# Hybrid encoder layer on one core: a new list of stage priorities for the list scheduler

## The chip, the core and the metric

The kernel runs on one core of a Trainium2 chip. A core has five engines that run their own instruction streams and meet at semaphores: PE (TensorE, matrix products; PEld are its weight loads), DVE (VectorE), ACT (ScalarE), POOL (GpSimd) and SP (SyncE, which here only issues transfers). Transfers between HBM and on-chip memory run on 16 DMA engines. The metric is the device time of one execution in microseconds (us), as a median over runs. The profile is one execution, recorded on the chip.

## What is computed

One encoder layer for 512 tokens of width 1024, everything in float32, cut to what matters:

```python
h = rmsnorm(x, mix_norm)
p = h @ w_in                                   # 1024 x 9248
rx, ry, qkv, z, ba, gates = split(p)
y_rnn = rglru_branch(rx, ry, ...) @ w_rnn_proj # gated linear recurrence, forward and backward, 1536 channels
y_dn  = deltanet_branch(qkv, z, ba, ...) @ w_dn_proj   # 8 heads, chunks of 64 tokens, both directions
g_rnn, g_dn = split(sigmoid(gates))
x = x + (g_rnn * y_rnn + g_dn * y_dn) @ w_out
h = rmsnorm(x, ffn_norm)
gt, up = split(h @ w_gate_up)                  # 1024 x 5632
x = x + (silu(gt) * up) @ w_down               # 2816 x 1024
return rmsnorm(x, final_norm)

# inside deltanet_branch, per head and chunk:
A   = strict_lower((k * beta) @ k.T * decay)
u   = solve(A + I, v * beta);  w = solve(A + I, kb * exp(gc))
# then a scan over the chunks with a 128 x 128 state
```

## The kernel before, in words

**Products.** Every large float32 product is made of three products of a reduced type (fp32r): each operand is split into a high part, cast by ACT (`whi`, `hh`), and a low part, the rest, subtracted by DVE (`wlo`, `hl`). PE then does high by high, high by low and low by high into one PSUM tile (`mm`, `st` or `ax`). So each block of 1024 x 128 weights costs one transfer into `wraw`, one ACT cast, one DVE subtraction and a few dozen matmuls, most of 512 columns. The feed-forward part (`gate_up`, L1350) works by a Strassen scheme in 20 units of 84 matmuls of 256 columns: it adds and subtracts weight blocks on DVE to save products on PE.

**The delta net** goes through four groups `g` of two heads. `dn_mats(g)` (L861) computes K by K products on PE (into an `ax` tile), and DVE writes the scaled triangular matrix into `na`. `dn_inverse(g)` (L901) inverts it: 69 DVE instructions that depend on one another (an elimination of 30 steps on 32 x 32 blocks), then on PE a dense batch of 32 x 32 matmuls (`pr`, `px`, `pz`) and of 64 x 64 ones, with ACT copies between. `dn_state(g)` (L985) goes over the chunks.

**Down projection ahead.** Ten of the Strassen units, and the plain unit before them, carry a `down_sums` (L1162): two transfers of `w_down` blocks, two DVE additions into `bg`, and one transfer of the sums back to HBM.

**What sets the order.** Nothing is issued while the Python runs. A `Plan` object (L52) records every instruction as an operation, with its engine, its estimated cost and its dependencies (`Plan.add`, L118). Calls of `spend(us)` (L439) open a new *stage*; there are 229, numbered from 0. Within a stage an operation has an offset of its own: for instance, a weight transfer is put 40 us ahead of the product that uses it. At the end `Plan.order()` (L145) makes one list of all operations by list scheduling: it steps through an estimated time, and each engine that is free takes the ready operation with the smallest key. The key is

```python
for (s, d), b in zip(self.where, self.bases):
    if s < len(TIMES):
        b, b0 = TIMES[s] * 100, b
    elif TIMES:
        b += max(TIMES) * 100 - b0
    when.append(b + d)
```

that is, `TIMES[stage] * 100` plus the offset, in ns. Stages past the end of the list keep their planned distances, behind the largest entry. On ACT a change of the function table adds `SWITCH` to the key. A key is only a rank among ready operations, not a time at which anything is meant to run. The keys also decide which tile gets a buffer first (`slots`, L187): the pools have 3 `wraw`, 2 `whi`, 2 `wlo`, 14 and 22 scratch tiles, 2 `bg` and 8 PSUM tiles.

The resulting list is emitted instruction by instruction, so that each engine's stream is fixed in that order; an engine waits where the next operand is not there. The emission has one line, so nearly every instruction of the profile carries L379, and the profile is read by tile names.

**Stages by number:** 0 to 2 norm and constants; 3 the beta and gate columns; 4 to 51 input projections, the recurrence and the first delta group's inputs, mixed; 60, 76, 92 and 110 `dn_mats` of groups 0 to 3, followed in 61, 77, 93 and 111 by `dn_inverse` and in 62, 78, 94 and 112 by `dn_state`; 125 to 141 the branch projections; 143 to 174 the output projection; 175 to 178 two plain feed-forward units; 179 to 198 the 20 Strassen units; 199 to 221 the down projection; 222 to 228 the last products, the final norm and the writes.

Of the kernel before, what the change touches and what calls it, by code (L numbers as in the profile page):

```python
# [32 lines left out]
RELEASE = 200  # L33
LOOK = 40
TIMES = [
# [10 lines left out]
]  # L46
ENGINES = ("PE", "DVE", "ACT", "POOL", "SP")
N2, N4, NW = 14, 22, 3
# [1575 lines left out]
```

## Time and profile before

| what | before |
|---|---|
| median of 3 runs | 1064.7 us (1064.27 to 1064.9) |
| the profiled execution: first to last instruction | 1066.3 us |
| granted TensorE clock, mean | 0.996 |
| PE busy | 1045.2 us (98%), 6731 matmul records |
| DVE busy | 867.6 us (81%), 1606 instructions |
| ACT busy | 675.7 us (63%), 1244 instructions |
| POOL busy | 53.0 us (5%) |
| HBM read and written | 113.78 MB and 7.90 MB |

The profiled execution's own time is its span: 1066.3 us, counted from the first to the last instruction, which stands 1.6 us above the median of the runs. In the views, a row of the timeline gives the start, the duration, the engine and the tiles (output<-inputs), with the idle time before it in brackets and what ended it. A row of the waits gives the waiting engine and tile, what was waited for, the sum in us, how often, and the longest. A row of the windows gives the stretch, its length, the busy time of each engine with the number of instructions, the granted clock of PE, the busy share of the DMA engines and the GB/s.

### The profile page before, as it was taken

To read this page: it belongs to the slowest core of one execution; us is meant where nothing else is said; L and a number is where in the kernel's file an instruction comes from. 1 tells how busy PE (TensorE), PEld (TensorE's weight loads), DVE (VectorE), ACT (ScalarE), POOL (GpSimd) and SP (SyncE) were. 2 spreads that over 40 slices of the span, in tenths; PEclk is the share of its full clock that TensorE was granted. 3 is DMA by queue.
4 is the path that set the end of the run, shared out by engine and by line. 5 is a ranking of instruction groups with operands and counts; after the bars stand their busy time and mean duration, and the time that the engine had idled before them with its cause. 6 is when DMAs were issued, how large, how long until landed. Compare 5 with 4: busy or idle time off the path is not lost.

```text
span 1066.3 us, 17661 instructions
## 1 busy us (share of the span) xinstructions
PE 1045.2 (98%) x6731; PEld 908.7 (85%) x6731; DVE 867.6 (81%) x1606; ACT 675.7 (63%) x1244; POOL 53.0 (5%) x109
## 2 busy tenths in 40 slices
PE   8999999999999999999999999999999999999997
PEld 7888888887879887988788898889999999998876
DVE  7679899669966696599379567669989989889998
ACT  7997997878464856783874534447444544546664
POOL 2000000202000211110020000000000000000000
PEclk9999999999999999999999999999999999999999
DMA  8142333224331243223203222554577433325643
GB/s 254 45 119 79 102 85 91 68 86 124 104 109 33 83 125 91 58 73 99 71 15 96 79 103 80 183 168 149 178 229 246 129 102 104 113 93 197 193 137 113
DMA packets 174390, 122.83 MB, mean 115 GB/s; under 512 B 5953, under 2 KB 160721, under 8 KB 174305
## 3 DMA queue, kind: packets, MB, share of 16 engines
q1 hardware_dynamic: 172832, 118.41, 37.1%
q10 hardware_dynamic: 1184, 3.15, 0.8%
q8 instruction: 53, 0.87, 0.3%
q0 software_dynamic: 288, 0.13, 0.1%
q14 instruction: 33, 0.26, 0.1%
HBM read 113.78 MB, written 7.90 MB: 114 GB/s over the span
## 4 chain that ended last, share of the span: by engine, by line
PE 71%; DVE 14%; ACT 8%; issue 4%; DMA 3%; POOL 0%; SPq 0%; DVEq 0%; ACTq 0%; POOLq 0%
PE mm L379 43%; PE ax L379 18%; PE st L379 10%; DVE t L379 9%; ACT t L379 5%; DVE wlo L379 3%; ACT L379 1%; DVE na L379 1%; ACT whi L379 1%; ACT ax L379 1%; DMA wraw<-sums 1%; DMA wraw<-in_w_in_dram 1%; DMA wraw<-in_w_gate_up_dram 1%; DMA bg<-in_w_down_dram 1%; DVE hl L379 0%
## 5 line engine op out<-in xcount | busy, mean ns | idle before, releaser
L379 DVE TENSOR_TENSOR t<-t,t 128x512 fp32r<-128x512 f32 (+23 forms) x466 | 226.7, 501 | 14.8 <-ACT t L379 6.3
L379 PE MATMUL mm<-hh,whi 128*128 128x512 f32 (+2 forms) x648 | 229.4, 363 | 0.4 <-ACT hh L379 0.4
L379 PE MATMUL mm<-hl,whi 128*128 128x512 f32 (+2 forms) x648 | 228.9, 362 | 0.8 <-DVE hl L379 0.8
L379 ACT CAST whi<-wraw 128x1024 fp32r<-128x1024 f32 (+3 forms) x139 | 130.1, 937 | 155.2 <-PE mm L379 87.8
L379 DVE TENSOR_TENSOR wlo<-wraw,whi 128x1024 fp32r<-128x1024 f32 (+3 forms) x138 | 150.4, 1092 | 75.1 <-PE mm L379 27.4
L379 PE MATMUL mm<-hh,wlo 128*128 128x512 f32 (+1 forms) x632 | 146.8, 364 | 0.0
L379 PE MATMUL ax<-t,t 32*32 32x32 f32 (+3 forms) x1062 | 141.7, 288 | 2.9 <-issue 1.8
L379 PEld LDWEIGHTS mm<-hl,whi 128*128 128x128 f32 (+1 forms) x648 | 121.8, 188 | 18.5 <-DVE hl L379 1.2
L379 PEld LDWEIGHTS mm<-hh,whi 128*128 128x128 f32 (+1 forms) x648 | 121.7, 188 | 17.8 <-ACT hh L379 0.7
L379 PEld LDWEIGHTS ax<-t,t 128*128 128x128 f32 (+1 forms) x1062 | 109.5, 162 | 20.9 <-issue 4.6
L379 PEld LDWEIGHTS mm<-hh,wlo 128*128 128x128 f32 x632 | 109.1, 190 | 17.4
L379 ACT CAST t<-t 128x512 fp32r<-128x512 f32 (+2 forms) x128 | 80.9, 650 | 48.2 <-DVE t L379 42.9
L379 DVE SCALAR_TENSOR_TENSOR t<-mm,par,t 128x511 f32<-128x511 f32 (+1 forms) x108 | 80.3, 745 | 20.3 <-ACT t L379 19.0
L379 PE MATMUL mm<-t,t 128*128 128x256 f32 (+1 forms) x468 | 91.6, 337 | 0.8 <-DVE t L379 0.7
L379 ACT ACT_TABLE_LOAD x69 | 88.5, 1283 | 5.2 <-PEq L1610 1.7
L379 PE MATMUL mm<-t,whi 128*128 128x512 f32 x320 | 82.1, 395 | 0.5 <-ACT whi L379 0.5
L379 PEld LDWEIGHTS mm<-t,t 128*128 128x128 f32 x468 | 72.4, 190 | 11.1 <-DVE t L379 2.5
L379 PEld LDWEIGHTS mm<-t,whi 128*128 128x128 f32 x320 | 59.3, 188 | 12.7 <-ACT whi L379 0.7
L379 ACT CAST t<-wraw 128x1024 fp32r<-128x1024 f32 (+1 forms) x51 | 44.9, 881 | 29.0 <-DMA wraw<-in_w_gate_up_dram 11.2
L379 ACT ACTIVATE t<-t 128x128 f32<-128x128 f32 (+4 forms) x86 | 47.1, 559 | 24.9 <-DVE t L379 23.6
L379 DVE TENSOR_TENSOR t<-wraw,t 128x1024 fp32r<-128x1024 f32 (+1 forms) x51 | 51.7, 1016 | 6.1 <-ACT t L379 5.9
L379 PE MATMUL mm<-t,wlo 128*128 128x512 f32 x160 | 43.3, 394 | 0.0
(210 smaller groups left out, 1702.9 us busy)
## 6 DMA issues: line engine op xcount, KB each, us to landing
wraw<-in_w_in_dram SPq DMA_DIRECT2D x72, 512.0 KB, 3.8
wraw<-in_w_gate_up_dram SPq DMA_DIRECT2D x44, 512.0 KB, 4.2
wraw<-in_w_rnn_proj_dram SPq DMA_DIRECT2D x16, 384.0 KB, 3.6
bg<-in_w_down_dram SPq DMA_DIRECT2D x11, 512.0 KB, 4.1
sums<-bg SPq DMA_DIRECT2D x11, 512.0 KB, 4.7
wraw<-sums SPq DMA_DIRECT2D x11, 512.0 KB, 4.6
wraw<-in_w_down_dram SPq DMA_DIRECT2D x22, 256.0 KB, 3.0
wraw<-in_w_down_dram SPq DMA_DIRECT2D x11, 512.0 KB, 3.7
```

Of the source, the lines that this page charges most:

```text
L379: self.plan.add(e, lambda: real(*a, **kw), outs, ins, cost, tail, table)
```

## The change

The list `TIMES` is replaced. Before, it has 159 entries, so the stages 159 to 228 follow in their written order. Now it has 229, one for each stage. Nothing else is edited: the 9027 operations (5962 on PE, 1599 on DVE, 1073 on ACT, 288 on SP, 105 on POOL), their dependencies, their costs and the buffers are the same, and so are the 69 table loads of ACT. What differs is the order of the operations in each engine's stream. Its rank in the stream changes for 4731 of the PE operations (by 24 places in the median, 936 at most), 1300 on DVE (median 3, at most 209), 781 on ACT (2, at most 119), 181 of the transfers on SP (1, at most 52) and 27 on POOL. The first 69 PE operations and the last 39 keep their places. The Strassen units, before in the order 179 to 198, now run on PE as 189, 181, 185, 180, 184, 183, 187, 182, 186, 191, 190, 179, 192, 193, 188 and 194 to 198; the plain stages ahead of them run as 175, 178, 177, 176.

```diff
@@ -33,16 +33,21 @@
 RELEASE = 200
 LOOK = 40
 TIMES = [
-    -153745, -118892, -151742, -141630, -118601, -110624, -115268, -33958, -18020, -66486, -73432, -37443, -49540,
-    -96427, -2932, -10005, 30002, -13238, -18669, -31954, -4105, -17443, -5460, -3043, 2712, -10454, -106272, -25215,
-    -4405, -4474, -71401, -45517, 19, 1569, 1252, 1710, 1882, 339, 401, 1179, -2583, -305, -1496, -196, 1112, 1851,
-    1959, 307, 4092, 1300, 529, 332, 4510, 2510, 3349, 5357, 4287, 2169, 5410, 5079, 763, 3042, 961, 6670, 7423, 7373,
-    2783, 3770, 2025, 3412, 3379, 3235, 20345, 1104, -10802, 17411, 3929, 3722, 2892, 9407, 7303, 6092, 4144, 1886,
-    6828, -574, 4313, 3500, 46801, 4839, 17251, 10665, 5201, 5557, 8565, 10448, 7663, 9776, 8817, 9530, 6893, 10173,
-    8675, 8905, 14395, 8478, 11813, 13557, 7061, 4883, 10223, 14152, 17479, 22403, 25604, 46524, 10407, 11086, 4254,
-    6633, 22198, 5785, 16088, 14508, 29479, 23444, 19346, 32109, 17263, 18476, 22224, 14415, 18037, 27950, 24857,
-    26606, 25131, 24094, 27198, 27785, 27886, 75164, 25980, 60246, 72215, 44135, 41284, 42337, 57022, 79854, 51295,
-    76593, 48471, 47016, 131010, 50337, 33889, 73977, 46063,
+    -187643, -118769, -184225, -128312, -118391, -104675, -104478, -23120, -15870, -23110, -75762, -33567, -65832,
+    -76122, -3898, -7649, 25691, -10178, -19113, -22967, -3811, -11633, -6497, -2841, 148740, -8099, -101370, -22707,
+    -3979, -4282, -57687, -185545, 309, 348, 1307, 1668, 1764, 346, 355, 1227, -2823, -89, -54, -2701, 1258, 1510,
+    1683, 330, 148741, 1306, 362, 871, 5352, 2144, 2087, 6673, 4666, 2328, 5953, 6265, 1119, 2270, 1286, 6904, 8023,
+    7987, 2361, 4158, 4110, 2438, 4151, 4171, 150700, 1304, -8129, 17067, 4866, 4724, 4070, 9627, 9965, 6661, 4408,
+    1868, 6925, -1068, 5276, 3872, 149771, 4834, 24940, 8285, 5418, 10243, 10288, 13809, 8136, 13810, 7693, 10431,
+    6950, 9019, 10144, 10447, 150818, 7963, 17851, 24038, 7059, 7976, 11670, 19735, 23318, 15751, 26911, 45043, 15500,
+    10447, 5709, 6727, 12186, 6742, 12376, 15760, 148145, 23367, 23741, 38728, 12594, 19299, 15789, 26999, 22983,
+    150263, 25473, 31030, 26455, 25771, 27976, 27863, 27953, 65091, 27599, 149845, 147917, 91616, 44392, 93098, 65695,
+    91791, 93924, 117507, 64849, 64847, 124890, 139778, 93858, 93705, 44538, 93883, 148045, 148140, 147804, 152581,
+    148371, 147799, 65766, 153334, 149771, 134730, 147799, 170565, 150338, 65241, 147834, 147978, 148036, 148060,
+    148000, 149446, 148402, 148148, 148666, 148621, 148402, 148311, 148806, 148653, 149632, 148076, 149353, 149149,
+    149446, 149587, 149698, 149771, 149829, 149932, 150028, 150071, 150138, 150175, 150246, 150314, 150356, 150466,
+    150471, 150599, 150624, 150648, 150096, 150530, 150730, 150773, 150823, 150875, 150924, 150924, 150978, 151436,
+    152351, 152363, 150633, 150761, 151395, 151490, 152140, 152366, 152542,
 ]
 ENGINES = ("PE", "DVE", "ACT", "POOL", "SP")
 N2, N4, NW = 14, 22, 3
```

The entries that belong to the delta net's matrix and inverse stages (counting from 0) are: stage 60 from 763 to 1119, 61 from 3042 to 2270; 76 from 3929 to 4866, 77 from 3722 to 4724; 92 from 5201 to 5418, 93 from 5557 to 10243; 110 from 10223 to 11670, 111 from 14152 to 19735. The entries from 159 on are new.

## Prediction

> **What bounds the kernel now.** I read the page's head first, then the windows, the waits of PE, and the timeline at the places that these point to.
>
> ```profile
> span 1066.3 us, 17661 instructions
> PE 1045.2 (98%) x6731; PEld 908.7 (85%) x6731; DVE 867.6 (81%) x1606; ACT 675.7 (63%) x1244; POOL 53.0 (5%) x109
> ```
>
> PE is busy for 98% of the span. A new order removes no matmul, so it can only work on PE's idle time, 1066.3 - 1045.2 = 21.1 us, and on time in which PE runs below full clock. The windows say where both lie (columns: stretch, length, busy time of PE, PEld, DVE, ACT, POOL, granted clock, DMA share, GB/s).
>
> ```profile
> 0.00:25.00 25.00, 19.78 (x147) 18.57 (x148) 19.61 (x48) 18.74 (x39) 7.39 (x21) 1.00 0.88 252
> 25.00:300.00 275.00, 273.17 (x1257) 225.23 (x1256) 230.21 (x336) 223.86 (x337) 16.44 (x28) 1.00 0.33 93
> 400.00:425.00 25.00, 22.91 (x217) 18.04 (x215) 16.82 (x44) 15.96 (x33) 3.22 (x6) 0.93 0.35 96
> 500.00:525.00 25.00, 23.21 (x314) 18.39 (x313) 13.46 (x23) 16.21 (x33) 0.00 (x0) 1.00 0.24 64
> 525.00:775.00 250.00, 249.78 (x1663) 218.68 (x1662) 189.35 (x393) 135.73 (x279) 5.42 (x14) 1.00 0.38 117
> 775.00:825.00 50.00, 48.02 (x394) 47.21 (x393) 47.19 (x86) 22.65 (x41) 0.00 (x0) 1.00 0.73 238
> 825.00:1000.00 175.00, 175.00 (x1273) 166.61 (x1272) 161.72 (x282) 89.69 (x156) 0.00 (x0) 1.00 0.42 130
> 1000.00:1066.00 66.00, 58.55 (x263) 47.39 (x261) 60.12 (x98) 40.35 (x66) 0.00 (x0) 0.96 0.41 136
> ```
>
> Length less PE's busy time gives the idle time: 5.2 us in the first 25 us, 1.8 to 300, 2.1 in 400 to 425, 1.8 in 500 to 525, 0.2 to 775, 2.0 in 775 to 825, none to 1000, and 7.5 at the end. Start and end are mostly latencies (first transfers, last norm and write), and both orders share the first 69 and the last 39 PE operations. The rest is 1.8 + 2.1 + 1.8 + 0.2 + 2.0 = 7.9 us. The waits of PE name it:
>
> ```profile
> PE ax L379 <- DVE t L379: 4.2, 4, 2.1
> PE ax L379 <- DMA gain1r<-in_mix_norm_dram: 3.0, 1, 3.0
> PE ax L379 <- issue: 1.8, 1, 1.8
> PE ax L379 <- DVE na L379: 0.7, 1, 0.7
> PE mm L379 <- DVE t L379: 0.7, 1, 0.7
> PE mm L379 <- ACT whi L379: 0.5, 1, 0.5
> ```
>
> The only wait for a transfer is the one at the start. The longest wait for DVE is at the inverse of group 1, and costs twice: once as idle time, once in clock.
>
> ```profile
> 417.39 0.70 DVE L379 STREAM_TRANSPOSE t<-t 128x512 f32<-128x512 f32 x1
> 418.15 0.75 PE L379 MATMUL ax<-t,na 32*32 32x32 f32 x64 [2.09 <-DVE t L379]
> ...
> 418.00:419.30 1.30, 1.15 (x66) 1.06 (x67) 0.09 (x1) 1.15 (x4) 0.00 (x0) 1.00 0.31 72
> 419.30:422.80 3.50, 3.50 (x71) 2.50 (x70) 0.00 (x0) 2.10 (x7) 0.00 (x0) 0.51 0.43 128
> 422.80:426.00 3.20, 3.20 (x44) 2.44 (x44) 0.00 (x0) 2.48 (x8) 0.00 (x0) 1.00 0.00 0
> ```
>
> PE stands still for 2.09 us and then has a granted clock of 0.51 for 3.5 us, which loses 3.5 x (1 - 0.51) = 1.7 us. So what an order can still win is about 7.9 + 1.7 = 9.6 us, 0.9% of the span; what it can lose has no such limit.
>
> **The change, part by part.** The sum is made against the profiled execution's 1066.3 us, which stands 1.6 us above the median of 1064.7; the differences are carried over as they are.
>
> *Work.* Operations, shapes, table loads and bytes are the same: 0 us. A PE order has a price only where something comes late, since a matmul has the same pitch wherever it stands:
>
> ```profile
> 276.83 26.97 PE mm L379 x119
> 835.93 2.88 PE mm L379 x24
> ```
>
> That is the chain's pitch: 26.97 / 119 = 0.227 us per matmul of 512 columns, 2.88 / 24 = 0.12 us per matmul of 256. The 4731 PE operations with a new rank cost nothing by themselves.
>
> *Inverse of group 1, the wait above.* Two chains start at the K by K products and meet at the first `pr` matmul: other matmuls on PE, and on DVE the last `na` instructions, the 69 of the inverse, and foreign ones between them. I counted both in the two instruction orders. PE: 162 matmuls before, 152 after, so PE arrives 10 x 0.227 = 2.3 us earlier. DVE: 12 foreign instructions before, 10 after; the two that go are a `wlo` subtraction of 768 columns and an addition of 512.
>
> ```profile
> 379.73 0.68 DVE t L379
> 380.41 1.57 DVE na L379 x4
> 381.98 0.87 DVE wlo L379
> ```
>
> By these rows they are worth 0.87 + 0.68 = 1.55 us. Thus the gap grows by 2.3 - 1.55 = 0.7 us. But the 0.68 us instruction that stands ahead of the four `na` ones here stands earlier after; if PE's products do not hold those `na` back, DVE starts that much sooner, and the gap grows by only 0.1 us. I take the middle, +0.4, with the ends +0.1 and +0.8. A gap above 2.09 us should be followed by half clock again, so that term stays at 0.
>
> The Trainium skill ("TensorE: Matmul & The Clock Gate", section "What's actually happening") says that the clock falls after at least one idle window of about 3.4 us, and that the window runs free, without a fixed start. By that rule a gap of 2.1 to 2.9 us keeps full clock and the sum would be 1.7 us lower; the trace disagrees, with 0.51 after 2.09 us.
>
> *Inverses of groups 0, 2 and 3.* The same counts: for group 0, PE's cover goes from 241 to 264 matmuls (+23 x 0.227 = +5.2 us) against 7 more foreign DVE instructions, which at the mean in the next row are 3.5 us; group 2, 207 to 226 matmuls, 28 foreign DVE instructions in both; group 3, 177 to 208 (+7.0 us) against 7 more on DVE.
>
> ```profile
> L379 DVE TENSOR_TENSOR t<-t,t 128x512 fp32r<-128x512 f32 (+23 forms) x466 | 226.7, 501 | 14.8 <-ACT t L379 6.3
> ```
>
> The cover grows more than the work at all three: 0 us, and nothing to win, as the waits list no other wait of that size there.
>
> *The gap of 1.79 us in group 2's dense batch.*
>
> ```profile
> 510.14 0.92 PE L379 MATMUL ax<-t,t 32*32 32x32 f32 x84
> 512.85 0.28 PE L379 MATMUL ax<-t,t 32*32 32x32 f32 x12 [1.79 <-issue]
> ```
>
> 96 matmuls of one batch are cut in two, and the profile names no releaser. The batch is issued at 0.92 / 84 = 0.011 us per matmul, far faster than any other stretch, so I read the gap as the instruction stream running dry. The batch stands four records later in PE's stream after (5744 for 5740), with the same instructions in it: I take 0, with the ends -1.8 (it falls elsewhere, into ordinary matmuls) and +1.8 (another batch is cut as well).
>
> *Feed-forward, 775 to 825.* Here PE waits 2.0 us in pieces of up to 1 us, DVE is busy 47.19 of 50 us, and the DMA share is 0.73.
>
> ```profile
> 783.95 0.69 DVE L379 TENSOR_TENSOR bg<-bg,bgb 128x512 f32<-128x512 f32 x1
> 784.55 0.69 DVE L379 TENSOR_TENSOR bg<-bg 128x512 f32<-128x512 f32 x1
> 788.30 0.86 PE L379 MATMUL ax<-t,t 128*128 128x256 f32 x5 [0.97 <-DVE t L379]
> ```
>
> After, the first nine Strassen units carry 8 sums instead of 9, so DVE has 2 x 0.69 = 1.4 us less to do there, and SP three transfers fewer to issue. Against that, counted by PE's rank, DVE must have issued 7 instructions more at the first Strassen unit (3.5 us at 501 ns), 3 more two units later, 1 fewer after four, and 3 fewer after six. DVE has 24% of its time idle ahead of this (189.35 of 250 us busy), so these can mostly be done earlier, where their inputs are there. The two roughly cancel: 0, with the ends -2.0 (all waits go) and +3.5 (nothing hides the seven). The sum that moves goes to a unit at 825 to 1000, where PE has no idle time at all beside 92% DVE.
>
> *Transfers.* 181 of SP's 288 move, by one place in the median. Weights are asked for 40 us ahead in every stage, and no weight is in the list of waits. 0; the bound above is in the rival below.
>
> *The small waits.* `na` at 248 us (0.7) and `whi` at 169 us (0.5): the demand on DVE and ACT by each PE rank is nearly equal in both orders, so +0.1, with the ends -1.2 and +1.2.
>
> *The end.* PE's last 39 operations and DVE's last 10 are unchanged, but ACT and DVE reach the first final norm stages somewhat earlier. There remain bits of "issue" like this one in the chain:
>
> ```profile
> 1059.04 0.56 issue
> ```
>
> I take -0.3, half of it, with the ends -0.6 and 0.
>
> Sum: 0.4 + 0 + 0 + 0 + 0.1 - 0.3 = +0.2 us on 1064.7: 1064.9 us.
>
> **The rivals.** The measurement can tell about 0.2% from no change, that is 2.1 us: faster means below 1062.6, slower above 1066.8.
>
> *Faster: the gap at group 1 closes far enough that the clock stays full.* The trace has a threshold between its two gaps: after the 2.09 us the clock fell, after the 1.79 us it did not:
>
> ```profile
> 510.00:513.00 3.00, 1.21 (x97) 0.96 (x96) 0.00 (x0) 1.32 (x4) 0.00 (x0) 1.00 0.09 25
> 513.00:516.00 3.00, 3.00 (x25) 2.19 (x17) 0.00 (x0) 2.70 (x7) 0.00 (x0) 1.00 0.02 5
> ```
>
> A gap shorter by 0.3 us would thus save 1.7 us more, and one that vanishes 2.1 + 1.7 = 3.8 us: 1064.9 - 0.4 - 3.8 = 1060.7. For it: DVE is the late one, and 12 of its instructions there are foreign.
>
> ```profile
> 382.00:418.00 36.00, 34.05 (x151) 27.86 (x149) 34.06 (x81) 19.92 (x33) 4.36 (x7) 1.00 0.43 117
> ```
>
> DVE is busy for 34.06 of these 36 us, so each foreign instruction that leaves shortens the chain by its whole length; four of 0.9 us would do it. Against: only two leave, and ten matmuls of cover go with them.
>
> *Slower, the other side: a second inverse is cut with a clock loss.* If DVE reaches the transpose of group 2 or 3 late (or the dense batch's gap there passes 2.1 us), PE stands for 2.1 us and then loses 1.7 us: 1064.9 + 3.8 = 1068.7. It decides from a delay of the DVE chain that exceeds PE's cover by about 2 us. For it: gaps of 2.09 and 1.79 us exist, and the batch at 512.85 needs only 0.3 us more. Against: the cover grows by 19 and 31 matmuls (4.3 and 7.0 us) at these two groups.
>
> *The change does nothing where it counts.* The streams differ, but every wait keeps its place and size: 1064.7. It is in the same class as the forecast.
>
> The Trainium skill ("Runtime: NRT & Kernel Launch", section "Instruction fetch mechanics") says that the fetch of instructions is mostly hidden. By that the 1.79 us gap has another cause, which the new order may or may not keep, so the sum could be 1.8 us lower; no row here tells the cause.
>
> **How the numbers follow.** Forecast and "does nothing", within 0.2%: 0.42. Faster (the clock at group 1, or the feed-forward waits and the cut batch together, -2.0 - 1.8): 0.31, as each needs one of the bounds to be reached. Slower (the second inverse, or the seven DVE instructions at +3.5 alone): 0.27, less, since the cover grows there. The predicted time is that of the forecast, 1064.9, whose own range is 1062.6 to 1066.8. For 8 in 10 I go to the two rivals' times, 1060.7 and 1068.7, and leave out one in ten beyond either.
>
> **What would show it.** In the changed kernel's profile: the wait "ax <- DVE t" of 2.1 us or somewhat more ahead of the first 32 x 32 batch near 418 us, with a clock of about 0.5 behind it; the "issue" gap near 513 us; waits of 1 us or less between 775 and 825 us; PE busy 1045 us, more by at most 1.7 us per loss of clock. I am wrong if there is a new wait above 1 us, above all for a transfer (`wraw`) or for `whi`, if the clock in the windows falls at another place, or if the gap at group 1 is gone.

## The result and the profile after

The changed kernel takes 1059.75 us (median of 7 runs, 1059.05 to 1061.46) against 1064.7 us: a ratio of 0.9958 with a 95% interval of 0.9945 to 0.9972, 0.42% faster. The forecast was 1064.9 us, and its range ended at 1060.7, about 1 us above what was measured. Over all executions listed in this study, 104 of the kernel before and 12 of the changed one, the means are 1065.0 and 1060.3 us, 4.7 us apart.

First a correction of the baseline. The text ahead of the prediction sets the span of the profiled execution against the times. The lists of this study give for each execution its time and its span, and the time is 1.7 us longer than the span. The profiled execution of before, with a span of 1066.3 us, thus took about 1068.0 us: it stands 3.3 us above the median, not 1.6. Only 4 of the 104 spans are as long, so part of what the prediction read from it was not typical. The profiled execution of the changed kernel took 1061.46 us and stands 1.7 us above its median.

The head of the page and the waits of PE in the changed kernel (code lines are shifted by five, so L384 is the former L379):

```profile
span 1059.7 us, 17669 instructions
PE 1044.6 (99%) x6731; PEld 909.9 (86%) x6731; DVE 872.0 (82%) x1606; ACT 676.7 (64%) x1244; POOL 56.0 (5%) x109
```

```profile
PE ax L384 <- DVE t L384: 2.0, 3, 1.2
PE ax L384 <- issue: 1.1, 1, 1.1
PE mm L384 <- ACT whi L384: 0.5, 1, 0.5
PE ax L384 <- DVE na L384: 0.2, 1, 0.2
```

PE's work is the same, 1044.6 for 1045.2 us. The waits for DVE's `t` fell from 4.2 to 2.0 us, the cut from 1.8 to 1.1, the wait for `na` from 0.7 to 0.2. The same stretches as before, with the same columns:

```profile
0.00:25.00 25.00, 20.63 (x137) 19.53 (x138) 18.40 (x45) 18.52 (x39) 6.81 (x21) 0.93 0.87 237
25.00:300.00 275.00, 273.93 (x1265) 226.25 (x1265) 229.70 (x330) 222.72 (x339) 18.05 (x28) 1.00 0.33 93
300.00:400.00 100.00, 100.00 (x723) 84.19 (x723) 74.35 (x159) 64.91 (x150) 15.31 (x26) 1.00 0.32 89
400.00:425.00 25.00, 23.80 (x290) 18.72 (x290) 16.70 (x43) 16.47 (x31) 0.61 (x2) 1.00 0.31 85
500.00:525.00 25.00, 23.76 (x327) 19.58 (x326) 14.05 (x23) 19.27 (x40) 2.09 (x2) 1.00 0.32 87
525.00:775.00 250.00, 249.95 (x1670) 219.46 (x1670) 194.67 (x401) 134.62 (x274) 5.22 (x12) 1.00 0.42 130
775.00:825.00 50.00, 50.00 (x418) 49.92 (x418) 50.00 (x92) 25.25 (x46) 0.00 (x0) 1.00 0.63 193
```

Idle time of PE from 25 to 300 us is 1.1 (1.8 before), none from 300 to 400, 1.2 in 400 to 425 (2.1), 1.2 in 500 to 525 (1.8), none in 775 to 825 (2.0). The clock is 1.00 where it was 0.93 before, at 400 to 425; in this execution it is 0.93 in the first 25 us instead. The timeline at group 1's inverse:

```profile
412.78 0.69 DVE L384 TENSOR_TENSOR t<-id,t 128x512 f32<-128x512 f32 x1
413.51 0.71 DVE L384 STREAM_TRANSPOSE t<-t 128x512 f32<-128x512 f32 x1
414.27 0.75 PE L384 MATMUL ax<-t,na 32*32 32x32 f32 x64 [1.20 <-DVE t L384]
```

The gap is 1.20 us, where 2.09 stood and 2.2 to 2.9 were forecast.

### The profile page after: what moved, and what is told of

Read it like the earlier page. It is cut to its first block, busy times and chain, and to the rows that moved or that the text cites. A ratio compares the mean times of both kernels' runs of the same rounds, so it can differ in the third digit from the quotient of the medians.

```text
span 1059.7 us, 17669 instructions
## 1 busy us (share of the span) xinstructions
PE 1044.6 (99%) x6731; PEld 909.9 (86%) x6731; DVE 872.0 (82%) x1606; ACT 676.7 (64%) x1244; POOL 56.0 (5%) x109
## 4 chain that ended last, share of the span: by engine, by line
PE 79%; ACT 8%; DVE 7%; DMA 3%; issue 2%; POOL 0%; SPq 0%; DVEq 0%; ACTq 0%; POOLq 0%
PE mm L384 49%; PE ax L384 20%; PE st L384 11%; ACT t L384 5%; DVE t L384 4%; ACT L384 2%; DVE na L384 1%; ACT whi L384 1%; DVE wlo L384 1%; DMA wraw<-in_w_in_dram 1%; DMA wraw<-in_w_gate_up_dram 0%; ACT ax L384 0%; DMA t<-in_x_dram 0%; DMA wraw<-in_w_down_dram 0%; DMA graw<-in_rg_wx_dram 0%
## 5 line engine op out<-in xcount | busy, mean ns | idle before, releaser
L384 DVE TENSOR_TENSOR t<-t,t 128x512 fp32r<-128x512 f32 (+19 forms) x466 | 227.7, 500 | 19.1 <-ACT t L384 10.8
L384 PE MATMUL mm<-hh,whi 128*128 128x512 f32 (+2 forms) x648 | 230.0, 364 | 0.4 <-ACT hh L384 0.3
L384 PE MATMUL mm<-hl,whi 128*128 128x512 f32 (+2 forms) x648 | 229.4, 363 | 0.8 <-DVE hl L384 0.8
L384 ACT CAST whi<-wraw 128x1024 fp32r<-128x1024 f32 (+3 forms) x139 | 129.9, 936 | 129.8 <-PE mm L384 79.1
L384 DVE TENSOR_TENSOR wlo<-wraw,whi 128x1024 fp32r<-128x1024 f32 (+3 forms) x138 | 150.1, 1088 | 70.0 <-ACT whi L384 31.7
L384 PE MATMUL mm<-hh,wlo 128*128 128x512 f32 (+1 forms) x632 | 147.0, 363 | 0.0
L384 PE MATMUL ax<-t,t 32*32 32x32 f32 (+3 forms) x1062 | 140.8, 285 | 1.6 <-issue 1.1
L384 PEld LDWEIGHTS mm<-hl,whi 128*128 128x128 f32 (+1 forms) x648 | 122.0, 188 | 17.9 <-DVE hl L384 1.2
L384 PEld LDWEIGHTS mm<-hh,whi 128*128 128x128 f32 (+1 forms) x648 | 122.0, 188 | 17.8 <-ACT hh L384 0.5
L384 PEld LDWEIGHTS ax<-t,t 128*128 128x128 f32 (+1 forms) x1062 | 109.4, 159 | 19.6 <-issue 2.9
L384 PEld LDWEIGHTS mm<-hh,wlo 128*128 128x128 f32 x632 | 109.1, 189 | 17.3
L384 ACT CAST t<-t 128x512 fp32r<-128x512 f32 (+2 forms) x128 | 81.9, 652 | 49.2 <-DVE t L384 47.3
L384 PE MATMUL mm<-t,t 128*128 128x256 f32 (+1 forms) x468 | 91.3, 336 | 0.1
L384 DVE SCALAR_TENSOR_TENSOR t<-mm,par,t 128x511 f32<-128x511 f32 (+1 forms) x108 | 79.3, 743 | 10.3 <-ACT t L384 9.1
L384 PE MATMUL mm<-t,whi 128*128 128x512 f32 x320 | 83.4, 396 | 0.5 <-ACT whi L384 0.5
L384 PEld LDWEIGHTS mm<-t,t 128*128 128x128 f32 x468 | 72.7, 190 | 9.3 <-DVE t L384 0.5
L384 PEld LDWEIGHTS mm<-t,whi 128*128 128x128 f32 x320 | 59.2, 188 | 13.5 <-ACT whi L384 1.1
L384 ACT ACTIVATE t<-t 128x128 f32<-128x128 f32 (+4 forms) x86 | 47.1, 558 | 27.7 <-DVE t L384 26.2
L384 ACT CAST t<-wraw 128x1024 fp32r<-128x1024 f32 (+1 forms) x51 | 44.9, 881 | 20.8 <-DMA wraw<-in_w_gate_up_dram 11.3
L384 DVE TENSOR_TENSOR t<-wraw,t 128x1024 fp32r<-128x1024 f32 (+1 forms) x51 | 51.3, 1007 | 4.3 <-ACT t L384 4.2
L384 PE MATMUL mm<-t,wlo 128*128 128x512 f32 x160 | 42.7, 393 | 0.0
```

Source lines behind the costliest of these rows:

```text
L384: self.plan.add(e, lambda: real(*a, **kw), outs, ins, cost, tail, table)
```

## The experiments

Two theories stood against each other: that the gain lies at the inverse of group 1 and in the clock behind it, or that it lies in the feed-forward and the end, whose priorities are new. Each of the edits below is against the kernel named; where nothing is said, the computation is unchanged.

**The kernel before, profiled again.**

> The kernel before, unchanged, profiled once more. If the profile before is a typical execution, it shows the same span of about 1066 us, the gap of about 2.1 us at the inverse of group 1 with half clock behind it (1.7 us lost), the cut batch of group 2 (about 1.8 us) and about 2.0 us of PE idle in the feed-forward. The rival: the half clock is a chance of that one execution, since 1066.3 us stands above the medians, and this profile shows a span of 1062 to 1064 us with full clock behind the gap.

Measured: 1064.51 us, ratio 1.0001 (0.9988 to 1.0014); profiled span 1064.8 us. The waits of PE, and two stretches:

```profile
PE ax L379 <- DVE t L379: 3.1, 3, 2.0
PE ax L379 <- issue: 1.5, 1, 1.5
```

```profile
400.00:425.00 25.00, 23.01 (x216) 18.11 (x214) 16.82 (x44) 15.95 (x33) 3.38 (x6) 0.93 0.36 97
500.00:525.00 25.00, 23.48 (x305) 18.24 (x304) 13.17 (x23) 15.04 (x30) 0.00 (x0) 0.93 0.24 64
775.00:825.00 50.00, 49.68 (x410) 49.08 (x409) 48.81 (x87) 24.17 (x44) 0.00 (x0) 1.00 0.75 245
```

The gap at group 1 and the half clock behind it are there again. The 2.0 us of the feed-forward are not: 0.3 us. And the clock falls a second time, in 500 to 525, behind a gap of only 1.5 us. So the gap is typical, and a threshold between gaps of 1.8 and 2.1 us does not exist. The feed-forward's loss comes in some executions only: it stands again, with 2.0 us, in the profile of the moved `wlo` below, whose feed-forward is that of the kernel before.

**The two halves of the list.** Early half:

```diff
-TIMES = [... 159 entries ...]
+TIMES = after's entries 0 to 158
```

> The first 159 entries of the new list alone: the order up to the branch projections is the changed kernel's (PE, DVE, ACT and POOL streams identical up to stage 124), the feed-forward and the down projection keep the written order. If the gain of 5 us lies in the delta net (gap at group 1 1.2 instead of 2.1 us, 1.7 us of clock, cut batch 1.15 instead of 1.8 us, small waits), this is 2.5 to 4 us faster than before. If it lies in the feed-forward (2.0 us of PE waits) and the end, it is within 1 us of before.

Measured: 1060.13 us, ratio 0.9958 (0.9945 to 0.9971): the whole gain, and more than the 2.5 to 4 us that were expected of the delta net. Late half:

```diff
-TIMES = [... 159 entries ...]
+TIMES = before's entries 0 to 158, then after's entries 159 to 228
```

> The new entries from stage 159 on behind the old ones: up to the branch projections the order is that of before, the feed-forward, the down projection and the end are the changed kernel's but for a few places. If the gain lies in the feed-forward and the end, this is 2 to 3 us faster than before, and the two halves add up to the 5 us. If it lies in the delta net, it is within 1 us of before.

Measured: 1065.12 us, ratio 1.0011 (1.0000 to 1.0022): no gain. With that the second theory falls: the 70 new entries, and the new order of the Strassen units, are worth nothing that can be measured by themselves.

**The write-back of the sums.**

```diff
-Q.dma_start(sums[j], r)
+(left out; the later read takes w_down's block itself)
```

> The kernel before with the write-back of the ten to eleven sums left out (the down projection reads a weight block of the same size instead, so the output isn't the layer's); DVE's work and all orders are the same. If the PE waits of 2.0 us between 775 and 825 us come from a late weight transfer (DVE waits 1.9 us for wraw at 778 us, 6.4 us after its issue), they shrink below 0.7 us and the time falls by 1.3 us or more. If they come from the amount of DVE work, they stay at about 2 us and the time stays within 0.5 us.

Measured: 1064.18 us, ratio 0.9998 (0.9986 to 1.0009).

```profile
775.00:825.00 50.00, 50.00 (x419) 50.00 (x418) 50.00 (x91) 25.51 (x46) 0.00 (x0) 1.00 0.58 180
```

PE's waits in that stretch are gone in this profile, but they are also nearly gone in the kernel before when it is profiled again, so this run decides nothing about their cause (more on it below). By the interval of the times, leaving the write-back out gains at most 0.14%.

**One DVE instruction moved at group 1.** In both kernels a `wlo` subtraction of 1.22 us stands inside the inverse's DVE chain. It is moved behind the chain's last transpose, to which PE waits:

```diff
     todo = plan.order()
+    todo.remove(4097)                            # the wlo subtraction
+    todo.insert(todo.index(2908) + 1, 4097)      # 2908: the last transpose
```

In the kernel before:

> The kernel before with one DVE instruction moved: the wlo subtraction of 1.22 us that stands ahead of the last transpose of group 1's inverse (416.25 us) is issued right behind that transpose; PE needs its result only at 430.9 us. If the gap and the clock behind it are worth what the profiles say, the gap falls from 2.1 to 0.9 us, the clock stays at 1.00 in 400 to 425, and the time falls by 1.2 + 1.7 = 2.9 us. The rival, that the clock's loss follows from something other than the gap's length, gives 1.2 us, and the rival that the gap hides behind something later gives 0.

Measured: 1064.21 us, ratio 0.9993 (0.9978 to 1.0008).

```profile
417.52 0.71 DVE L379 STREAM_TRANSPOSE t<-t 128x512 f32<-128x512 f32 x1
418.15 1.18 DVE L379 TENSOR_TENSOR wlo<-wraw,whi 128x1024 fp32r<-128x1024 f32 x1
418.28 0.75 PE L379 MATMUL ax<-t,na 32*32 32x32 f32 x64 [1.08 <-DVE t L379]
```

```profile
400.00:425.00 25.00, 23.92 (x255) 19.15 (x255) 18.03 (x47) 16.63 (x35) 3.23 (x6) 1.00 0.42 111
500.00:525.00 25.00, 23.16 (x306) 18.06 (x305) 11.89 (x21) 15.25 (x30) 0.00 (x0) 0.93 0.25 64
```

The gap is 1.08 us and the clock there stays full, as expected, but in this profile it falls behind the cut in group 2's batch. Of the expected 2.9 us, 0.7 came, with an interval that holds both nothing and 2.3. It isn't shown that the loss went from one place to the other: in the second profile of the kernel before the clock falls at both, and the profile here is the slowest of its twelve executions. Over the twelve, (1 - mean clock) x span is 3.4 us on average, for 3.5 in the kernel before, so the gain in clock did not come. In the changed kernel:

> The changed kernel with the same instruction (there at 409.08 us) issued behind the last transpose of group 1's inverse, PE needs it at 420.7 us. The gap of 1.2 us at 414 us goes away: 1.2 us less, and no change of the clock, which is at 1.00 there already. The rival: PE waits for the moved wlo instead, or for the ACT copies behind the transpose, and nothing is gained.

Measured: 1059.45 us, ratio 0.9952 (0.9936 to 0.9969); the gap is 0.16 us. By the ratios that is 0.6 us below the changed kernel (0.9958), well within the intervals; a comparison on one chip follows below.

**POOL's instructions inside the inverse.** Comparing the two traces instruction by instruction, I found elimination steps on DVE that took 0.65 us instead of 0.25, each while a POOL instruction ran. In the kernel before:

```profile
388.76 1.14 POOL L379 TENSOR_SCALAR_AFFINE_SELECT t<-t 128x512 f32<-128x512 f32 x1 [7.84 <-ACT t L379]
389.31 0.65 DVE L379 TENSOR_TENSOR t<-t,t 128x30 f32<-128x30 f32 x1
```

and the same step, with two more, in the changed kernel, where that POOL instruction runs elsewhere:

```profile
387.91 0.73 DVE L384 TENSOR_TENSOR t<-t,t 128x30 f32<-128x30 f32 x3
```

Three steps in 0.73 us there, one in 0.65 us here. Two experiments, one that takes POOL's work out of the inverse and one that puts more in:

```diff
+late = [3571, 3590, 3597, 4513, 4514]           # three selects, two memsets
 for i in todo:
+    if i in late: continue
     plan.ops[i][1]()
+    if i == 2908:
+        nc.gpsimd.tensor_scalar(gate, <the transposed tile>[:, 0, 0:1], ...)   # POOL waits for the transpose
+        for k in late: plan.ops[k][1]()
```

> The kernel before with five POOL instructions (three selects of group 2's matrices, two memsets) held back until the last transpose of group 1's inverse; DVE's and PE's streams are the same. If a POOL instruction lengthens the DVE instruction that it meets by 0.4 us (a 0.25 us elimination step took 0.65 to 0.71 us at four places), three such hits go away, the DVE chain is 1.2 us shorter, and the gap falls from 2.1 to 0.9 us, with 1.7 us of clock behind it. If POOL has nothing to do with those durations, the gap stays at 2.0 to 2.1 us and the time within 0.5 us.

Measured: 1063.44 us, ratio 0.9981 (0.9966 to 0.9996).

```profile
402.76 1.22 DVE L379 TENSOR_TENSOR wlo<-wraw,whi 128x1024 fp32r<-128x1024 f32 x1
416.12 0.75 PE L379 MATMUL ax<-t,na 32*32 32x32 f32 x64 [0.68 <-DVE t L379]
```

```profile
400.00:425.00 25.00, 24.32 (x284) 19.39 (x282) 15.99 (x42) 18.58 (x37) 3.97 (x8) 1.00 0.32 85
500.00:525.00 25.00, 23.43 (x313) 18.56 (x312) 10.83 (x15) 17.74 (x39) 0.00 (x0) 0.93 0.21 57
```

The gap falls from 2.09 to 0.68 us with PE's and DVE's streams unchanged. The DVE chain from the last `na` to the last transpose takes 34.7 us instead of 36.1: two elimination steps of 0.6 us or more are left of four, and a `wlo` subtraction that runs beside selects in the kernel before is short again. Steps beside the two memsets kept their 0.28 us in the kernel before too. There the `wlo` was:

```profile
403.24 1.27 POOL L379 TENSOR_SCALAR_AFFINE_SELECT t<-t 128x512 f32<-128x512 f32 x2 [1.64 <-DMA t<-gcr]
403.94 1.65 DVE L379 TENSOR_TENSOR wlo<-wraw,whi 128x1024 fp32r<-128x1024 f32 x1
```

The opposite, in the changed kernel:

```diff
     plan.ops[i][1]()
+    if i == 2850:                                # an early step of group 1's elimination
+        nc.gpsimd.memset(scr, 0.0); nc.gpsimd.tensor_scalar(scr[:, 0:1], <the inverse's input>, ...)
+        for _ in range(10): nc.gpsimd.affine_select(out=sv, in_=sv, ...)   # sv: scr, read by nothing
```

> The changed kernel with ten more selects of 128x512 on POOL, back to back from about 386 us, inside group 1's inverse, on a tile that nothing reads. If POOL's instructions lengthen DVE's by 0.4 us each, the DVE chain is 3 to 4 us longer, the gap at 414 us is 4 to 5 us instead of 1.2, the clock falls behind it, and the time rises by 4 to 6 us. If not, the gap stays at 1.2 us and the time within 0.5 us.

Measured: 1066.92 us, ratio 1.0015 to before (0.9999 to 1.0031), against 0.9958 for the changed kernel without it.

```profile
386.36 7.96 POOL L1609 TENSOR_SCALAR_AFFINE_SELECT scr<-scr 128x512 f32<-128x512 f32 x10
388.82 5.60 DVE L384 TENSOR_TENSOR t<-t,t 128x56 f32<-128x56 f32 x8
416.05 0.88 PE L384 MATMUL ax<-t,na 32*32 32x32 f32 x64 [4.68 <-DVE t L384]
```

```profile
400.00:425.00 25.00, 20.32 (x233) 15.77 (x231) 15.98 (x44) 12.11 (x26) 0.61 (x2) 0.93 0.31 85
```

Eight steps take 5.60 us, where the changed kernel alone has:

```profile
390.41 2.10 DVE L384 TENSOR_TENSOR t<-t,t 128x56 f32<-128x56 f32 x8
```

The 3.5 us more come out one for one as PE's gap (4.68 for 1.20), and the clock falls behind it. That POOL slows DVE is shown. The Trainium skill ("GPSIMD Engine Reference", section "1. Specifications") says that GpSimd shares its SBUF interfaces with VectorE, with contention for DVE instructions that have two SBUF inputs; the elimination steps are of that kind, and the runs agree: 0.4 us per meeting.

**Both edits at group 1, in the kernel before.** The moved `wlo` and the five POOL instructions held back, together:

> The kernel before with both edits at group 1's inverse: the wlo of 1.22 us behind the last transpose, and the five POOL instructions held back until then. The gap of 2.1 us should be gone (below 0.3 us in 400 to 425), and the time 2.1 us lower for it and up to 1.7 us more for the clock, so 2 to 4 us below before. If the changed kernel's 5 us came mostly from other places (small waits up to 400 us, feed-forward), this gains 1 us or less.

Measured: 1061.77 us, ratio 0.9975 (0.9963 to 0.9987), 2.7 us.

```profile
400.00:425.00 25.00, 25.00 (x287) 19.94 (x285) 16.82 (x44) 18.58 (x37) 4.81 (x8) 1.00 0.35 92
500.00:525.00 25.00, 23.67 (x322) 18.88 (x321) 10.74 (x14) 19.50 (x50) 0.00 (x0) 1.00 0.28 75
```

PE has no idle time at all in 400 to 425. Two edits at one place, with no new list, give more than half of what the new list gives, by the medians.

**The changed kernel again, and the swap beside it.**

> The changed kernel, unchanged, profiled once more: a gap of about 1.2 us at group 1 with full clock behind it, a cut batch of 1.1 to 1.6 us, no PE wait of more than 0.3 us between 775 and 825 us, and 4.9 us less than before in the median.

Measured: 1060.81 us, ratio 0.9962 (0.9948 to 0.9977), 4.0 us less than before where 4.9 were expected. The gap is 0.93 us, the cut 1.36, PE's idle time in 775 to 825 0.15 us.

> The changed kernel with the wlo of group 1's inverse behind the last transpose, beside the changed kernel itself: the gap of 1.2 us is 0.2 us or less, so 0.5 to 1.0 us below the changed kernel if that gap is all on the path, the same if something behind it takes the time up again.

Measured: 1058.73 us, ratio 0.9944 (0.9929 to 0.9958). PE has no idle time in 400 to 425. Both kernels ran on the same chip beside the same runs of before, and each of the six executions with the swap (1058.07 to 1059.26) is shorter than each of the five without it (1059.61 to 1061.37). So the gap was on the path. The difference of the medians, 2.1 us, is more than the gap's 0.9; the listed clocks differ by 0.8 us of it on average, and the rest is open.

**The cut in group 2's dense batch.** Counted over weight loads, matmuls and the semaphore instructions between them, both kernels resume behind the cut with the same record of PE's stream, number 6081 (from 0), though the batch starts four records later in the changed one (84 and 12 matmuls before, 82 and 14 after). All 14 profiles with nothing added to PE's stream show it there. The changed kernel with 128 PE records more ahead of it:

```diff
     plan.ops[i][1]()
+    if 2915 <= i <= 2946: plan.ops[i][1]()       # group 1's 32 pr products twice
```

> The changed kernel with group 1's 32 products pr issued twice (the second time with the same result), which puts every later PE instruction 128 records further on in the stream, at 0.75 us of PE time. If the cut in group 2's dense batch belongs to a place in PE's instruction stream (in both kernels it stands ahead of the same record, number 6081 counting weight loads and matmuls), it moves away from 82 and 14 matmuls: 64 matmuls earlier, to about 18 and 78, or out of the batch's busy part altogether. If it belongs to the data (a product that waits for a tile), it stays at 82 and 14.

```profile
506.60 1.02 PE L384 MATMUL ax<-t,t 32*32 32x32 f32 x96
```

```profile
500.00:525.00 25.00, 24.91 (x341) 20.88 (x340) 13.73 (x20) 21.50 (x44) 1.65 (x2) 1.00 0.28 78
```

The batch of 96 runs through, and the idle time of the stretch is 0.1 us. Nothing that the batch reads was changed, so the cut does not come from its data. This is one execution, of 1058.04 us. One "issue" wait is left, in group 3's batch, and it stands at the same place in the last kernel below, which repeats these products too:

```profile
599.42 0.22 PE L384 MATMUL ax<-t,t 32*32 32x32 f32 x2 [0.47 <-issue]
599.64 0.22 PE L384 MATMUL ax<-t,t 32*32 32x32 f32 x2 [0.77 <-issue]
```

By the same count this is record 7617, 1536 behind 6081. Record 6081 itself now lies 18 matmuls into group 2's batch and does not stop it. So the stop goes with places in the instruction stream, but a place alone isn't enough; how densely the records ahead of it are issued may matter, which was not tried. The Trainium skill ("Runtime: NRT & Kernel Launch", section "Instruction fetch mechanics") calls the cost of a block boundary mostly hidden; if the stop is such a cost, then 1.1 to 1.8 us of it showed in both profiles of either kernel, in a stretch that issues a matmul every 0.011 us.

**What is left outside group 1.** The two edits at group 1 with the late half of the list:

> The two edits at group 1's inverse together with the new entries from stage 159 on; up to stage 124 only those two edits separate it from before. If the rest of the changed kernel's gain, beyond the 2.7 us of the two edits alone, comes from the feed-forward and the end, this is 4 to 5 us below before. If it comes from the small waits and the clock ahead of 550 us, it stays at about 2.7 us.

Measured: 1063.3 us, ratio 0.9983 (0.9970 to 0.9995). The late half adds nothing that can be measured to them either (0.9975 without it; the intervals overlap). With the early half's 0.9958 that puts the rest of the gain ahead of it, in the order up to the branch projections.

**The best of what was found.** The changed kernel with the swap and the repeated `pr`:

> The changed kernel with both edits that helped it: the wlo behind group 1's last transpose (gap of 0.9 us gone) and group 1's pr issued twice, so that the cut in group 2's dense batch (1.1 to 1.6 us) falls elsewhere in the stream. If both are on the path: 0.9 + 1.3 - 0.75 = about 1.5 us below the changed kernel, 6 to 7 us below before. If the shift only moves the cut to another dense stretch, about 0.2 us below it.

Measured: 1058.43 us, ratio 0.9938 (0.9926 to 0.9949), the fastest kernel here, 6.6 us below before by the ratio and 2 us or more below the change. Against the swap alone (0.9944) the intervals overlap, so the second edit isn't shown to be worth its 0.75 us of work.

## Why the prediction was wrong, point by point

**What bounds the kernel: right.** PE's work did not change, and the gain is idle time and clock. From the listed executions, clock lost is (1 - mean clock) x span: 3.5 us on average before, 2.4 after. So about 1.1 us of the 4.7 is clock, and 3.6 us are waits. This is a rough split, since it counts the half clock of the last few us too, where PE mostly stands still.

**The baseline: wrong.** The span was set against the median of the times, without the 1.7 us between them. It made an unusually slow execution look ordinary, and with it a loss of 2.0 us in the feed-forward that only some executions have.

**The inverse of group 1: the step that failed.** Forecast was a gap larger by 0.4 us, with ends at +0.1 and +0.8; it is smaller by 0.9. Measured part by part from the two traces: PE's cover between the last K by K product and the first `pr` shrank by 2.2 us (forecast 2.3, right). The `na` instructions start 1.0 us earlier against PE: not one instruction but two had stood ahead of them, and both moved (0.68 and 0.75 us; the first `na` now waits 0.44 us for PE, so 1.0 us is left; forecast 0.34, end 0.68). The foreign instructions in the chain shrank from 12.1 to 10.4 us (1.65, forecast 1.55). And the inverse's own 69 instructions, which the forecast held constant, went from 24.3 to 23.6 us. By its ends the whole DVE chain from the last `na` to the transpose shrank by 2.1 us (a little less than these sums, since neighbouring rows overlap): 2.2 - 1.0 - 2.1 = -0.9, the measured change. The own instructions are faster because POOL runs beside fewer of them: two steps of 0.6 us or more are left of four. So two terms of the step failed, `na` at 0.34 us for 1.0, and the inverse's own instructions at nothing for 0.7. The text ahead of the prediction counts 27 POOL instructions with a new place, and the prediction gave them no price; the two POOL experiments show it, 0.4 us for each meeting.

**The other inverses: right.** No wait above 0.3 us for DVE at groups 0, 2 and 3 in the changed kernel.

**The clock: the term was wrong.** The forecast kept it at 0, on a threshold between gaps of 1.79 and 2.09 us read from one profile. The profiles of this study hold gaps of 1.5, 1.5, 1.6 and 1.8 us behind which the clock fell at group 2, and others of 1.6, 1.6, 1.7 and 1.8 us behind which it did not; at group 1 it fell behind 1.6, 2.0, 2.1 and 4.7 us, and not behind 1.7 us, nor behind any of 1.2 us or less. So the length of a gap does not decide it. The traces show most of what does. In each of the 16 profiles the clock changes only on a grid of 3.41 us, which lies elsewhere in each execution, and each half clock between two full ones lasts one step of it. Here are steps of that grid, five from the kernel before and two from its second profile, with the same columns as above:

```profile
415.92:419.34 3.42, 1.33 (x67) 1.10 (x67) 2.17 (x3) 1.99 (x6) 0.00 (x0) 1.00 0.13 31
419.34:422.75 3.41, 3.41 (x70) 2.41 (x70) 0.00 (x0) 2.01 (x7) 0.00 (x0) 0.50 0.43 127
508.08:511.49 3.41, 2.98 (x154) 2.29 (x140) 1.74 (x3) 3.18 (x9) 0.00 (x0) 1.00 0.62 159
511.49:514.91 3.42, 2.06 (x20) 1.44 (x19) 0.00 (x0) 1.65 (x5) 0.00 (x0) 1.00 0.02 5
514.91:518.32 3.41, 3.41 (x41) 2.69 (x41) 2.09 (x3) 2.58 (x5) 0.00 (x0) 1.00 0.00 0
510.63:514.04 3.41, 1.89 (x100) 1.60 (x86) 0.00 (x0) 1.76 (x6) 0.00 (x0) 1.00 0.02 6
514.04:517.45 3.41, 3.41 (x10) 2.17 (x9) 0.88 (x2) 3.04 (x6) 0.00 (x0) 0.50 0.00 0
```

The gap of 2.09 us lies within one step, and the next step has half clock. The gap of 1.79 us is cut by the grid into 0.43 and 1.36 us, and the clock stays full. The gap of 1.52 us in the second profile lies within one step, and the clock falls. Between 400 and 550 us all eight falls of the 16 profiles come behind a step with 1.52 us or more of idle time, and no step with 1.46 us or less has one behind it. One step shows that idle time alone isn't the whole rule: in the kernel with ten selects more, 1.70 us at the end of a step (409.67 to 413.08 us) cost nothing, and the 2.97 us of the next step did. So the forecast asked for the length of the gap, where the runs show its share of one step; for a gap of 1.5 to 2 us that is a matter of luck in each execution. The rule of the Trainium skill that the prediction quoted ("TensorE: Matmul & The Clock Gate", section "What's actually happening") has two parts: the window that runs free fits these traces, but an idle window of about 3.4 us does not fit as a limit on the gap, as 1.5 us were enough.

**The cut batch: right in place, and 0 was a fair value.** It stayed ahead of the same record. It measured 1.2 and 1.4 us in the two profiles of the changed kernel, 1.8 and 1.5 in those of before, 0.4 us less on average. Over all profiles the two ranges overlap (1.15 to 1.57 us in the new order, 1.33 to 1.84 in the old one). The places 5740 and 5744 that the prediction gives are those of the batch of 64 ahead of the cut one.

**The feed-forward: 0 holds as far as the times of the late half tell, its reason does not.** The late half alone gave no gain. But the prediction argued from PE's waits that no weight is late. DVE's own waits in the kernel before show one, in the profile already there:

```profile
DVE t L379 <- DMA wraw<-in_w_gate_up_dram: 1.9, 1, 1.9
```

DVE was busy for 94% of that stretch, so there was little room to make its wait up before PE needed its results. The other profiles agree: where DVE waits for this transfer for 2.2, 1.9, 1.5, 1.1, 1.0, 0.9, 0.6 and 0.3 us between 770 and 800 us, PE is idle for 2.0, 2.0, 1.2, 0.5, 0.6, 0.3, 0.2 and 0.0 us between 775 and 825. The last two are the changed kernel's. Where DVE has no such wait, in six other profiles, PE is not idle there. No experiment separates the cause, but the waits of an engine that is nearly full must be read like PE's.

**The small waits: mis-sized.** Forecast +0.1 us. From 25 to 400 us, PE's idle time is 2.0 us before and 1.6 in its second profile, and 1.1 and 0.9 in the two of the changed kernel, 0.8 us less on average. The wait for `na` at 248 us is 0.5 us of it: 0.7 us in both profiles of before, 0.2 in both of the changed kernel. The whole is about the size of what the two edits at group 1 leave over: on the same chip they stand 1.0 us above the changed kernel by the medians. The clock is no part of that rest, since (1 - mean clock) x span averages 2.1 us with the two edits and 2.4 in the changed kernel. Which move made which small wait go was not tried.

**The end: right in sign, mis-sized.** Forecast -0.3 us, with the ends -0.6 and 0. From 1045 us to the end PE is idle for 7.5 us in both profiles of before and 6.8 in both of the changed kernel:

```profile
1045.00:1066.32 21.32, 13.80 (x70) 11.61 (x68) 16.60 (x37) 9.49 (x23) 0.00 (x0) 0.88 0.28 99
1045.00:1059.72 14.72, 7.95 (x44) 6.77 (x42) 10.79 (x30) 8.49 (x21) 0.00 (x0) 0.88 0.40 144
```

The 0.7 us come with the late half: its own profile has 6.8 us as well, and that of the early half 7.5. The times of the late half alone do not show this gain. In its profile PE is idle for 1.0 us between 825 and 1045 us, where it was 0.25 before; whether that takes it up was not tried.

**The rival that came true** was "faster: the gap at group 1 closes". Its place was right and its mechanism half: the gap closed by 0.9 us and not by 2.1. That the time nevertheless came near the rival's 1060.7 us is in part luck: fewer falls of the clock, smaller waits and a shorter end, none of them the rival's terms in this size, made up for the rest of the gap.

## What to carry to other kernels

An engine that is off the path can still lengthen the one that is on it: when a reordering moves POOL instructions into or out of a chain of short DVE instructions, price each meeting, and compare the durations of the same instruction in other surroundings before holding them constant. Set a profile's span against the spans of other executions, not against their times, and profile the kernel before twice when the effect looked for is below half a per cent. Where one place holds most of the avoidable time, moving one or two instructions there by hand can give most of what a search over all priorities gives, and it adds to it.

## What was not expected of the hardware

One POOL instruction of 0.6 to 1.1 us lengthens a DVE step of 0.25 us by 0.4 us, and ten back to back lengthen eight steps from 2.10 to 5.60 us. PE's clock changes only on a grid of 3.41 us that lies elsewhere in each execution, and fell behind gaps as short as 1.5 us where a gap lay within one step of it. A batch of 96 small matmuls stops for 1.1 to 1.8 us at one place of the instruction stream, and runs through when the stream is shifted by 128 records; a shorter stop then stands 1536 records further on.
